# Eight chunks' loads, issued from GpSimd's queue instead of SP's: a hybrid decoder block

## The chip, the cores and the metric

The kernel runs on one core of one Trainium2 chip. The metric is the time of one execution on the device in microseconds (us), median of several runs. The core has five engines with a queue of instructions each: TensorE (PE in the profile, its weight loads PEld), VectorE (DVE), ScalarE (ACT), GpSimd (POOL) and SyncE (SP). A transfer between HBM and SBUF is issued by an instruction on one of the queues and carried out by 16 DMA engines. SBUF is the memory that the engines work in, PSUM the one that TensorE writes to.

## The reference

One layer over 2048 positions of width 1024, all in float32:

```python
h = rmsnorm(x, norm1_g[l])
proj = h @ w_in[l]
p_q, p_k, p_v, p_g, p_a, c_b, c_c, c_h = jnp.split(proj, splits, axis=-1)
...
o = gla_chunked(q, k, v, log_a)              # gated linear attention, 4 heads
o = rmsnorm(o, gla_norm_g[l]).astype(x.dtype)
o_gla = (o * jax.nn.silu(p_g...)).reshape(bsz, seq, GLA_WIDTH)
u = c_c * c_h
o_conv = c_b * causal_depthwise_conv(u, conv_w[l])
mixed = jnp.concatenate([o_gla, o_conv], axis=-1) @ w_out[l]
x = x + mixed
h2 = rmsnorm(x, norm2_g[l])
ffn = (jax.nn.silu(h2 @ w_ffn_gate[l]) * (h2 @ w_ffn_up[l])) @ w_ffn_down[l]
return rmsnorm(x + ffn, norm_f_g)
```

The attention works on chunks of positions. In each chunk q and k are scaled with exponentials of the summed log decays, scores of q and k are masked and multiplied with v, and a state (per head 64 x 128) is carried from chunk to chunk:

```python
q_i = q * jnp.exp(b)
k_i = k * jnp.exp(-b)
scores = jnp.where(causal, jnp.einsum('nbhck,nbhsk->nbhcs', q_i, k_i), 0.0)
o = jnp.einsum('nbhcs,nbhsv->nbhcv', scores, v) + jnp.einsum('nbhck,nbhkv->nbhcv', q_i, state_prev)
```

## The kernel before

Positions are cut into four blocks of 512 (`PB`), two to a half. Large products run on operands split into a high and a low part (`split`, lines 206 and 207: ACT rounds to the high part, DVE subtracts for the low one), three matmuls for one (lines 504 to 506), and by a scheme with seven block products for eight (`PRODUCTS`, `unit`). Weights come in as `raw` tiles and are added, split into `wq` tiles (four buffers) and multiplied.

The stages in order: the input projection of half 0, that of half 1, the first output projection (`first_out_proj`, half 0), the second (`out_proj`, half 1), then the feed-forward part for both halves.

Attention runs beside the projections. The kernel uses chunks of 128 positions, eight to a half. The input projection writes q and k, the summed log decays, v and the gate of each chunk to scratch tensors in DRAM (`s_kq`, `s_d`, `s_v`, `s_g`). `gla_half(half)` is a generator which fetches them back and works through the chunks; each call of `tick()` in the projections takes one of its steps. A chunk goes through these steps:

- `gla_fetch` (line 1156) takes four tiles `kq`, `ee`, `vt`, `gt` from the pool `bx`, and issues four loads through `load` (line 156), which is SP's queue: ee (128 KB), kq, vt and gt (256 KB each).
- `gla_scaled` takes two exponentials on ACT (lines 1163 and 1164) and scales k and q on DVE (1165 and 1166).
- `gla_scores` makes the scores on TensorE (1176) and masks them on DVE (1179), and transposes k and v (1182, 1185).
- `gla_outputs` multiplies (1201, 1208), makes the chunk's share of the state (1216 on TensorE, 1226 and 1227 on DVE) and the norm, and scales the outputs into a tile `osb` of the same pool (1242).
- `gla_finish` transposes, multiplies with the gate (1252), splits and stores to `s_gla` (line 1257).

The pool `bx` has 11 buffers (line 74). Chunk n+1 is fetched behind the scores of chunk n and ahead of the finish of chunk n-1. The tile `gt` is held until the finish; `kq`, `ee` and `vt` are free after lines 1208 and 1216.

The second half's chunks are fetched from the later part of half 1's input projection on, through `first_out_proj`. There the operands of the output projection are loaded too (`mix_operands`, line 1316: tiles `op`), with weights (`raw`), residuals (`y`, line 1339) and stores of results, all on SP's queue. In `first_out_proj` each product is added to the residual on DVE (`plus`, line 1366), and the first two rows of results are squared on ACT (`sum_squares`, line 1271).

No order is written down for most of this. The program is traced in the order of the Python code, which sets priorities, and a planner then orders each queue at build time by a model's times and hands out buffers and semaphores (line 1965):

```python
with _tile.TileContext(nc, schedule_with_timeline_sim=True) as tc:
    tile_hymba_block(tc, *args)
```

At run time each queue is carried out in the planned order; an instruction waits for its semaphores, and what stands behind it waits too. Some places fix an order by hand (`behind`, `tc.issue_after`, `queued`), among them the table load ahead of the first chunk (line 1130).

GpSimd's queue holds ten multiplications at the very end (line 1739) and a few fills at the start, and no DMA.

Of the kernel before, what the change touches and what calls it, by code (L numbers as in the profile page):

```python
# [54 lines left out]
def tile_hymba_block(ctx, tc, x, xt, win, wa, wgu, wout, wffn, wdown, wdown_first, small, out):  # L55
    nc = tc.nc
    act, dve, pool, pe = nc.scalar, nc.vector, nc.gpsimd, nc.tensor
# [95 lines left out]
    def bt(name, shape=(P, PB)):  # L153
        return bx[0].tile(list(shape), F32, name=name, tag="b")

    def load(dst, src):
        return nc.sync.dma_start(dst, src)
# [970 lines left out]
    def gla_half(half):  # L1128
        chunks = [(b, t) for b in (2 * half, 2 * half + 1) for t in range(PT)]
        with tc.issue_after(last_silu[0].ins):  # L1130
            tables = act.preload_act_table_set("natural_log_exp_and_others")
        fetched = gla_fetch(*chunks[0])
        yield
        with tc.issue_after(tables.ins):
            cur = gla_scaled(*fetched)
        yield
        o = None
        for n, (b, t) in enumerate(chunks):
            s = gla_scores(b, t, *cur)
            yield  # L1140
            if n + 1 < len(chunks):
                fetched = gla_fetch(*chunks[n + 1])
            if o is not None:
                yield from gla_finish(*chunks[n - 1], *o)
            o = gla_outputs(b, t, *s)
            if n + 1 < len(chunks):
                cur = gla_scaled(*fetched)
            yield
        yield from gla_finish(b, t, *o)
        done.add((b, t))  # L1150
        yield
# [4 lines left out]
    def gla_fetch(b, t):  # L1156
        kq, e, vt, g = [bt(n, (P, 4, P)) for n in ("kq", "ee", "vt", "gt")]
        for dst, src in ((e[:, 2:4, :], s_d), (kq[:], s_kq), (vt[:], s_v), (g[:], s_g)):
            load(dst, src[b][:, t])
        return kq, e, vt, g  # L1160

    def gla_scaled(kq, e, vt, g):
# [807 lines left out]
```

## Time and profile before

| | |
|---|---|
| median of 3 runs | 2032.9 us (2032.5 to 2035.67) |
| the profiled execution | 2031.92 us, its span 2030.0 us |
| granted TensorE clock, mean | 0.997 |
| busy: PE, PEld, DVE, ACT, POOL | 2011.4, 1654.4, 1564.8, 973.1, 10.3 us |
| DMA | 425.12 MB, mean 209 GB/s; all but 5 issues of the program on SP's queue |
| loads of the chunks (both halves) | kq, vt, gt: 16 issues each of 256 KB, landing after 4.7, 4.7 and 4.8 us (medians); ee: 16 of 128 KB, 4.8 us |

Times in the profile count from the first instruction. A line of a timeline gives start, duration, engine, line of the code, operation, `out<-in` by the program's names, and the count of instructions merged into it; a bracket behind it is idle time of that engine and what ended it. `SPq` marks an issue on SP's queue, whose duration is that of issuing; the time to landing is given apart. A line of a table by stretches gives for each engine its busy time and count, then the granted clock as a share (PEclk), the mean busy share of the 16 DMA engines (it can come out a little above 1), and GB/s. In the view of waits, `A <- B: total, times, longest` says how long A stood idle until B released it. In the view of a tile, three numbers are the smallest, the median and the largest duration in ns.

### The profile page before, as it was taken

Reading aid. Unit: us, or ns where it says so; the run is one execution under the profiler, and the core shown is the slowest. Engines: PE = TensorE matmul, PEld = TensorE weight load, DVE = VectorE, ACT = ScalarE, POOL = GpSimd, SP = SyncE. Lnnn points to the kernel's source line nnn. Section 1 sums busy time; section 2 is a strip of 40 time slices with the busy share of each in tenths; the row PEclk is TensorE's granted clock in tenths of the full one; section 3 lists DMA queues with packets and bytes.
Section 4 is the critical chain, followed back from the end, with each engine's and each line's share of the span. In section 5 each row is a group of like instructions: output and inputs, shape, how many; then the busy total and the mean of one; then the engine's idle time right before and its main releaser. Section 6 shows DMA issues by size and latency. Waiting matters only on the chain.

```text
span 2030.0 us, 26783 instructions
## 1 busy us (share of the span) xinstructions
PE 2011.4 (99%) x9275; PEld 1654.4 (81%) x9275; DVE 1564.8 (77%) x2837; ACT 973.1 (48%) x1941; POOL 10.3 (1%) x17
## 2 busy tenths in 40 slices
PE   9999999999999999999999999999999999999998
PEld 8888888788878888888888888887888888888886
DVE  7888868677867877877876687887767767778886
ACT  6664455754544444444444552334434444454345
POOL 0000000000000000000000000000000000000001
PEclk9999999999999999999999999999999999999999
DMA  7366876654777863545544676586444434586653
GB/s 264 117 200 215 288 278 207 184 171 138 262 272 256 293 232 130 181 169 199 182 163 174 233 283 246 186 286 268 171 151 171 174 132 171 183 331 217 249 218 130
DMA packets 191943, 425.12 MB, mean 209 GB/s; under 512 B 17760, under 2 KB 67136, under 8 KB 182336
## 3 DMA queue, kind: packets, MB, share of 16 engines
q1 hardware_dynamic: 191088, 422.76, 59.1%
q8 instruction: 73, 1.20, 0.2%
q10 hardware_dynamic: 720, 0.66, 0.1%
q14 instruction: 62, 0.51, 0.1%
HBM read 277.60 MB, written 145.75 MB: 209 GB/s over the span
## 4 chain that ended last, share of the span: by engine, by line
PE 96%; DMA 1%; DVE 1%; ACT 1%; issue 0%; SPq 0%; POOL 0%; POOLq 0%; DVEq 0%; ACTq 0%
PE mm L504 27%; PE mm L506 27%; PE mm L505 27%; PE mm L1395 1%; PE mm L1437 1%; PE mm L1439 1%; PE mm L1436 1%; PE a_ps L1028 1%; PE mm L809 1%; PE mm L811 1%; PE mm L810 1%; PE o_ps L1201 1%; PE mm L1401 1%; PE mm L1756 1%; PE sc L1176 1%; PE o_ps L1208 1%
## 5 line engine op out<-in xcount | busy, mean ns | idle before, releaser
L504 PE MATMUL mm<-op,wq 128*128 128x512 f32 x2499 | 973.0, 392 | 2.2 <-ACT c L550 1.4
L505 PE MATMUL mm<-op,wq 128*128 128x512 f32 x2499 | 972.0, 390 | 0.1
L506 PE MATMUL mm<-op,wq 128*128 128x512 f32 x2499 | 961.2, 390 | 0.3
L206 ACT ACTIVATE wq<-raw 128x512 fp32r<-128x512 f32 (+2 forms) x628 | 361.9, 581 | 596.3 <-PE mm L506 487.0
L504 PEld LDWEIGHTS mm<-op,wq 128*128 128x128 f32 x2499 | 469.0, 188 | 105.1 <-ACT wq L206 2.5
L506 PEld LDWEIGHTS mm<-op,wq 128*128 128x128 f32 x2499 | 469.1, 188 | 99.1 <-DVE wq L207 1.1
L505 PEld LDWEIGHTS mm<-op,wq 128*128 128x128 f32 x2499 | 469.2, 188 | 97.4 <-DVE op L207 2.0
L207 DVE TENSOR_TENSOR wq<-raw,wq 128x512 fp32r<-128x512 f32 (+2 forms) x628 | 390.1, 626 | 150.6 <-ACT wq L206 149.2
L538 DVE TENSOR_TENSOR c<-mm,c 128x512 f32<-128x512 f32 x196 | 134.7, 687 | 76.4 <-PE mm L506 71.4
L538 DVE TENSOR_TENSOR y<-mm,y 128x512 f32<-128x512 f32 x185 | 126.5, 686 | 52.0 <-PE mm L506 51.6
L550 ACT ACTIVATE c<-mm 128x512 f32<-128x512 f32 x198 | 115.6, 588 | 28.8 <-PE mm L506 26.2
L456 DVE TENSOR_TENSOR raw<-raw 128x512 f32<-128x512 f32 (+2 forms) x190 | 116.6, 619 | 2.1
L206 ACT ACTIVATE wq<-s 128x512 fp32r<-128x512 f32 (+2 forms) x100 | 58.0, 580 | 110.3 <-PE mm L506 96.5
L456 DVE TENSOR_TENSOR s<-raw 128x512 f32<-128x512 f32 (+2 forms) x95 | 58.9, 620 | 28.0 <-DMA raw<-in_wffn_dram 18.6
L207 DVE TENSOR_TENSOR op<-op 128x512 fp32r<-128x512 f32 x108 | 70.6, 682 | 1.9 <-ACT op L206 1.9
L206 ACT ACTIVATE op<-op 128x512 fp32r<-128x512 f32 x108 | 63.1, 621 | 10.1 <-DMA op<-sa_T 4.4
L207 DVE TENSOR_TENSOR wq<-s,wq 128x512 fp32r<-128x512 f32 (+2 forms) x100 | 62.4, 624 | 1.8 <-ACT wq L206 1.0
L456 DVE TENSOR_TENSOR raw<-s,raw 128x512 f32<-128x512 f32 (+2 forms) x95 | 59.0, 621 | 1.4
L605 ACT ACTIVATE sg<-mm 128x512 f32<-128x512 f32 x26 | 15.5, 597 | 87.6 <-PE mm L506 87.6
L605 ACT ACTIVATE c<-c 128x512 f32<-128x512 f32 x78 | 48.9, 628 | 13.0 <-DVE c L538 10.4
L1436 PE MATMUL mm<-op,wq 128*128 128x512 f32 x128 | 50.0, 392 | 0.0
L1437 PE MATMUL mm<-op,wq 128*128 128x512 f32 x128 | 49.8, 389 | 0.0
(238 smaller groups left out, 1665.4 us busy)
## 6 DMA issues: line engine op xcount, KB each, us to landing
raw<-in_wffn_dram SPq DMA_DIRECT2D x44, 1024.0 KB, 6.6
sa_B<-so SPq DMA_DIRECT2D x47, 512.0 KB, 4.1
op<-sa_B SPq DMA_DIRECT2D x47, 512.0 KB, 7.0
raw<-in_win_dram SPq DMA_DIRECT2D x22, 1024.0 KB, 5.7
sa_T<-so SPq DMA_DIRECT2D x44, 512.0 KB, 4.4
op<-sa_T SPq DMA_DIRECT2D x44, 512.0 KB, 6.8
raw<-in_wdown_dram SPq DMA_DIRECT2D x24, 768.0 KB, 5.5
sx<-y SPq DMA_DIRECT2D x48, 256.0 KB, 3.6
```

What stands on the lines that cost most here:

```text
L206: last_hi[:] = [act.activation(hi, src, AF.Copy)]
L207: last_lo[:] = [dve.tensor_tensor(lo, src, hi.bitcast(F32), ALU.subtract)]
L456: dve.tensor_tensor(*args)
L504: pe.matmul(o[:], wh, xh, start=first and k == 0, stop=False, skip_group_check=True)
L505: pe.matmul(o[:], wh, xl, start=False, stop=False, skip_group_check=True)
L506: return pe.matmul(o[:], wl, xh, start=False, stop=k == n - 1, skip_group_check=True)
L538: last_plus[:] = [dve.tensor_tensor(t[:], o[:], t[:], ALU.add)]
L550: last_out[:] = [act.activation(t[:], o[:], AF.Copy)]
L605: last_silu[:] = [act.activation(s[:], c[:], AF.Silu)]
L809: pe.matmul(acc[:], wq[:, 0, c], p[:, 0, :], start=first, stop=False)
L1436: pe.matmul(o[e, j][:], wh, m[:, 0, :], start=n == 0, stop=False)
L1437: pe.matmul(o[e, j][:], wh, m[:, 1, :], start=False, stop=False)
```

## The change

In `gla_fetch` the four loads of a chunk of blocks 2 and 3, the second half, are issued with `pool.dma_start`, on GpSimd's queue. The first half's stay on SP's. That is 32 of the 64 chunk loads. Tiles, sources and the place in the traced program are the same; the planner makes its order anew.

```diff
@@ -1156,7 +1156,10 @@
     def gla_fetch(b, t):
         kq, e, vt, g = [bt(n, (P, 4, P)) for n in ("kq", "ee", "vt", "gt")]
         for dst, src in ((e[:, 2:4, :], s_d), (kq[:], s_kq), (vt[:], s_v), (g[:], s_g)):
-            load(dst, src[b][:, t])
+            if b < 2:
+                load(dst, src[b][:, t])
+            else:
+                pool.dma_start(dst, src[b][:, t])
         return kq, e, vt, g
```

## The prediction, on record before the changed kernel ran

> **What bounds the kernel now.** I read the page first: the span, the busy times and the chain that ended last.
>
> ```profile
> span 2030.0 us, 26783 instructions
> PE 2011.4 (99%) x9275; PEld 1654.4 (81%) x9275; DVE 1564.8 (77%) x2837; ACT 973.1 (48%) x1941; POOL 10.3 (1%) x17
> PE 96%; DMA 1%; DVE 1%; ACT 1%; issue 0%; SPq 0%; POOL 0%; POOLq 0%; DVEq 0%; ACTq 0%
> ```
>
> TensorE holds 96% of the chain and is busy for 2011.4 of 2030.0 us. A moved load can therefore pay only where TensorE stands still, 18.6 us in all, and only in the part of it that the second half's chunks cause. So next came a table by stretches over the time in which these chunks run, within 460 to 645 us.
>
> ```profile
> core 0: us, PE busy (x) PEld busy (x) DVE busy (x) ACT busy (x) POOL busy (x), PEclk, DMA share, GB/s
> 500.00:536.00 36.00, 36.00 (x208) 29.34 (x207) 28.12 (x64) 23.60 (x63) 0.00 (x0) 1.00 0.43 133
> 536.00:556.00 20.00, 20.00 (x114) 16.33 (x113) 18.18 (x44) 10.17 (x31) 0.00 (x0) 1.00 0.99 380
> 556.00:570.00 14.00, 14.00 (x77) 11.21 (x76) 9.75 (x25) 5.12 (x19) 0.00 (x0) 1.00 1.05 398
> 570.00:575.00 5.00, 0.67 (x3) 0.21 (x2) 4.52 (x11) 3.09 (x7) 0.00 (x0) 0.98 1.00 351
> 575.00:580.00 5.00, 4.88 (x24) 4.23 (x25) 1.57 (x5) 1.82 (x4) 0.00 (x0) 0.68 1.08 392
> 580.00:600.00 20.00, 20.00 (x111) 15.99 (x110) 13.73 (x33) 8.27 (x25) 0.00 (x0) 1.00 0.69 223
> ```
>
> One hole shows, at 570 to 575, and behind it a stretch of 5 us at a granted clock of 0.68. Before and after, TensorE is full at clock 1.00. From 536 to 580 the DMA engines are full too (share 0.99 to 1.08): the operands of the first output projection come in there. The view of waits, over 460 to 645 us, for TensorE alone and then for all engines:
>
> ```profile
> PE sc L1176 <- DVE kq L1166: 4.4, 1, 4.4
> ```
>
> ```profile
> ACT ee L1163 <- DMA ee<-sd: 5.7, 4, 3.9
> DVE kq L1165 <- DMA kq<-sk: 4.7, 3, 2.1
> ```
>
> The hole is one wait of the scores of a chunk (the sixth of the second half) for its scaled q and k. Chunk loads do keep ACT (5.7 us) and DVE (4.7 us) waiting as well, but TensorE has no hole at those places, so there these waits cost nothing.
>
> **What ends the one hole.** The timelines of the four engines, put in order of time:
>
> ```profile
> 570.06 0.61 PE L1401 MATMUL mm<-op,wq 128*128 128x512 f32 x2
> 571.46 1.28 DVE L1366 TENSOR_TENSOR y<-mm,y 128x512 f32<-128x512 f32 x2
> 572.17 1.23 ACT L1271 ACTIVATE ssx<-y 128x512 f32<-128x512 f32 x2 [1.04 <-DVE y L1366]
> 573.44 0.42 ACT L206 ACTIVATE wq<-raw 128x256 fp32r<-128x256 f32 x1
> 573.76 0.40 ACT L1163 ACTIVATE ee<-ee 128x256 f32<-128x256 f32 x1
> 574.19 0.42 ACT L1164 ACTIVATE ee<-ee 128x256 f32<-128x256 f32 x1
> 574.23 0.42 DVE L1165 TENSOR_TENSOR kq<-kq,ee 128x256 f32<-128x256 f32 x1
> 574.64 0.42 DVE L1166 SCALAR_TENSOR_TENSOR kq<-kq,ee 128x256 f32<-128x256 f32 x1
> 575.12 1.23 PE L1176 MATMUL sc<-kq 64*128 64x128 f32 x8 [4.44 <-DVE kq L1166]
> ```
>
> ```profile
> 566.50 0.32 SPq L157 DMA_DIRECT2D ee<-sd  x1
> 567.24 0.32 SPq L157 DMA_DIRECT2D kq<-sk  x1
> ```
>
> The ee load, issued at 566.50, landed after 4.9 us, and kq's, issued at 567.24, after 6.5 us, by the view of each tile held to these two issues:
>
> ```profile
> DMA to landing us min/median/max: 4.9/4.9/4.9
> ```
>
> ```profile
> DMA to landing us min/median/max: 6.5/6.5/6.5
> ```
>
> So ee was there at 571.4 and kq at 573.7, both before their first reader (573.76 and 574.23). No row of the chain carries a wait for a DMA. What TensorE waits for is the order on ACT and DVE: two residual additions (L1366) that need its last product, two squares (L1271), one weight split (L206), and only then the exponentials (L1163, L1164) and the scaling (L1165, L1166).
>
> **What the change removes.** 8 chunks by 4 loads, 32 issues on SP. Medians from the views of the tiles:
>
> ```profile
> L157 SPq DMA_DIRECT2D ee<-sd x16: 319/524/1668, 288.9 to 593.4; - x16
> L157 SPq DMA_DIRECT2D kq<-sk x16: 319/404/646, 289.6 to 593.8; - x16
> ```
>
> With the two other loads at kq's price that is 0.52 + 3 x 0.40 = 1.7 us a chunk, 14 us of SP over 130 us. SP is not on the chain (0%), so the saving itself is worth nothing. What stood behind these loads on SP (operand loads, weights, stores of finished chunks) goes out sooner. No TensorE wait ends on one of those either, so this too counts 0; the cover is TensorE's full stretches above.
>
> **What it moves.** On SP a chunk's loads stand in program order behind everything else. The sixth chunk's come out at 566.50, though the products that last read the buffers of the fourth chunk's ee, kq and vt end near 548.3:
>
> ```profile
> 547.00 0.71 PE L1208 MATMUL o_ps<-carry,kq 64*128 64x128 f32 x8
> 547.65 0.66 PE L1216 MATMUL kv<-vt,ee 128*64 128x128 f32 x8
> ```
>
> If the planner gives the sixth chunk these buffers, GpSimd can issue its loads from about 548 on: estimated 18 us earlier. The bytes stay the same and the 16 engines are full, so the loads overtake other traffic and make no room.
>
> ```profile
> kq<-sk SPq DMA_DIRECT2D x16, 256.0 KB, 4.7
> ee<-sd SPq DMA_DIRECT2D x16, 128.0 KB, 4.8
> ```
>
> Three loads of kq's size and ee are 0.9 MB; at 398 GB/s they put 2.3 us in front of operands already queued. Those are read by products in a stretch where TensorE shows no wait; I take 0, and 2.3 us as the other end.
>
> **What it adds.** 32 issues on GpSimd, and for each consumer a wait on a semaphore of another queue. GpSimd has nothing else between these two rows:
>
> ```profile
> 1.41 0.41 POOL L83 TENSOR_SCALAR_AFFINE_SELECT mask<-mask 128x256 f32<-128x256 f32 x1
> 2014.19 7.06 POOL L1739 TENSOR_TENSOR y<-y,ssx 128x512 f32<-128x512 f32 x7 [2012.38 <-ACT ssx L1733]
> ```
>
> No row shows a load issued there. The nearest are its own operations, 0.41 us and 7.06/7 = 1.01 us. Then ee and kq are out after 0.8 to 2.0 us, against 0.9 us on SP, and all four after 1.6 to 4.0 us. [...] Where a chunk has no lead, 1.1 us (2.0 less 0.9) would show. Queued behind a waiting load on GpSimd are only loads of later chunks, until 2014 us.
>
> [...]
>
> **The sum.** The profiled execution took 2031.92 us (span 2030.0), 1 us below the median of three runs, 2032.9. Removed from the path 0, moved 0, added 0: while ACT and DVE keep their order, the wait of 4.44 us stays, since an earlier kq waits in SBUF until ACT comes to L1163. That gives 2031.92 for this execution and 2032.9 us for the median. About 0.2%, 4.1 us, is what a measurement of this kernel can tell from no change.
>
> **Rival: the planner moves the exponentials forward (faster).** The order on every queue is planned when the program is built, from a model's times, and a load on an idle queue has another time in it. ACT has room ahead of the hole:
>
> ```profile
> 569.58 0.73 ACT L206 ACTIVATE wq<-raw 128x256 fp32r<-128x256 f32 x2 [2.37 <-PE mm L506]
> ```
>
> The two exponentials (0.82 us) fit into these 2.37 us of idle, DVE has 4.25 us free in 556 to 570 for the scaling, and TensorE would go on at 570.67. Gone are 4.44 us and the slow clock behind it, 5.00 x (1 - 0.68) = 1.6 us: 6.04 us, 2026.9 us. For it: the loads can come 18 us earlier. Against: full DMA engines hold back the modelled arrival too, whichever queue issues.
>
> **Rival: another order, another hole (slower).** Scores are placed with no reserve: the fifth chunk's ran at 548.24, one tenth of a microsecond after its scaling.
>
> ```profile
> 547.73 0.41 DVE L1166 SCALAR_TENSOR_TENSOR kq<-kq,ee 128x256 f32<-128x256 f32 x1
> 548.24 0.71 PE L1176 MATMUL sc<-kq 64*128 64x128 f32 x8
> ```
>
> If the new plan counts on earlier loads and puts the scores of the fifth or seventh chunk further forward, while DVE (18.18 of 20 us busy in 536 to 556) gets to the scaling as late as now, TensorE stops there as it does at 570. It decides from the point where the scores come up before the end of L1166. Each such stop, priced as the one there is, costs 6.04 us: 2038.9, and 2045.0 with two. For it: DVE is the second busiest engine and just there nearly full. Against: the present plan has only one such stop in eight chunks.
>
> **Rival: GpSimd in DVE's way (slower).** The end of the kernel is the one place where both work on SBUF:
>
> ```profile
> 2011.03 0.17 DVE L1708 TENSOR_TENSOR rs<-py 128x4 f32<-128x4 f32 x1 [0.45 <-ACT py L1705]
> 2015.45 1.29 DVE L1708 TENSOR_TENSOR rs<-py 128x2 f32<-128x2 f32 x1
> ```
>
> The same operation took 0.17 us alone and 1.29 us beside GpSimd's products, 1.12 us more. At that price for each load, the 8 loads of the fifth and sixth chunks cost DVE 9.0 us; 1.8 us are idle in 536 to 556, and the other 7.1 us would reach TensorE: 2040.0 us. Against: GpSimd reads tensors at 2015 and would not for a load.
>
> [...]
>
> **How the numbers follow.** No change to speak of, 2032.9: 0.29. Exponentials forward, 2026.9: 0.26. New holes, 2038.9 to 2045.0: 0.27. GpSimd against DVE, 2040.0 or worse: 0.18. Forecast 2032.9 us, its own range 2032.5 (the lowest run) to 2035.2 (2.3 us for overtaken operands). With the others: from 2026.0, the lowest run 2032.5 less 6.04, rounded down, to 2045.0; a third hole or a dearer GpSimd lies outside. Faster 0.26, same 0.29, slower 0.45.
>
> **What would show it.** Right, if the 32 loads stand on GpSimd's queue, the waits of ACT and DVE for ee and kq shrink from 5.7 and 4.7 us to near nothing, the sixth chunk's loads land many microseconds before L1163, and TensorE still waits some 4.4 us for L1166 behind the two L1271. Wrong to the fast side, if L1163 stands ahead of L1271 and the hole and the 0.68 stretch are gone. Wrong to the slow side, if there are more waits of sc for kq, if operations of DVE are stretched while GpSimd issues, or if a landing from GpSimd's queue takes clearly longer than 4.9 to 6.5 us.

## The result and the profile after

The changed kernel takes 2037.84 us, the kernel before 2032.57 us (medians of 16 executions each). The ratio is 1.0023, 95% interval 1.0017 to 1.003: slower by 5 us. The ratio on record is an estimate of its own and not the quotient of the medians, which is 1.0026; so it is with the ratios below. Three slow executions, of 2547.07, 5402.24 and 6934.36 us, are left out of all medians and ratios below. The forecast was 2032.9 us, no change, with 2032.5 to 2035.2 as its own range. The executions of the changed kernel also lie further apart, 2034.25 to 2041.9 us, where 14 of the 16 of the kernel before lie within 2031.45 to 2033.6. The profiled execution of the changed kernel took 2034.3 us, one of its shortest, so its trace shows only a part of the loss; two more executions were profiled for that reason. Behind `gla_fetch` the line numbers are 3 higher than before.

The page of the changed kernel, its span, busy times, DMA queues and the chain:

```profile
span 2032.6 us, 26832 instructions
...
PE 2013.0 (99%) x9275; PEld 1656.8 (82%) x9275; DVE 1565.8 (77%) x2837; ACT 973.5 (48%) x1941; POOL 27.5 (1%) x49
...
q0 software_dynamic: 2304, 7.34, 1.2%
q8 instruction: 73, 1.20, 0.2%
...
q14 instruction: 64, 0.52, 0.1%
...
PE 97%; DVE 1%; DMA 1%; ACT 1%; issue 0%; POOL 0%; POOLq 0%; SPq 0%; ACTq 0%
```

The 32 loads are a queue of their own now (q0). Two more queues matter below, of the kind that the page calls `instruction`: q8 with packets of 16 KB (1.20 MB / 73) and q14 with packets of 8 KB (0.52 MB / 64). They are read here as fetches of the engines' instructions.

The table by stretches, to be set against the one of before:

```profile
536.00:556.00 20.00, 19.16 (x106) 14.99 (x105) 17.35 (x41) 9.91 (x29) 1.60 (x3) 1.00 0.99 384
556.00:570.00 14.00, 14.00 (x78) 11.18 (x77) 9.93 (x27) 5.46 (x18) 2.05 (x4) 1.00 1.05 393
570.00:575.00 5.00, 1.96 (x9) 1.30 (x7) 3.88 (x9) 2.90 (x7) 0.09 (x1) 1.00 1.00 387
575.00:580.00 5.00, 3.82 (x20) 3.22 (x21) 3.49 (x9) 2.34 (x6) 0.54 (x1) 0.73 0.75 262
```

The one hole of before is still there, and so is the slow clock behind it (0.73). The order that makes it is the one foreseen, here from the timelines of ACT, DVE and TensorE:

```profile
572.90 0.63 ACT L1274 ACTIVATE ssx<-y 128x512 f32<-128x512 f32 x1 [0.48 <-DVE y L1369]
573.83 0.63 ACT L1274 ACTIVATE ssx<-y 128x512 f32<-128x512 f32 x1 [0.30 <-DVE y L1369]
574.50 0.42 ACT L206 ACTIVATE wq<-raw 128x256 fp32r<-128x256 f32 x1
574.82 0.40 ACT L1166 ACTIVATE ee<-ee 128x256 f32<-128x256 f32 x1
...
575.70 0.42 DVE L1169 SCALAR_TENSOR_TENSOR kq<-kq,ee 128x256 f32<-128x256 f32 x1
576.18 0.71 PE L1179 MATMUL sc<-kq 64*128 64x128 f32 x8 [4.22 <-DVE kq L1169]
```

The sixth chunk's loads are out 18 us earlier (GpSimd's timeline). They land after 6.2 us (ee) and 7.0 us (kq), at 554.8 and 556.4 us, 20 and 19 us ahead of their readers. Over the whole second half the median time to landing is shorter than before, but most loads are issued at other times (the view of DMA from 430 to 645 us, first the changed kernel, then the one before):

```profile
548.55 0.54 POOL L1162 DMA_DIRECT2D ee<-sd  x1 [22.74 <-PE o_ps L1211]
549.35 0.54 POOL L1162 DMA_DIRECT2D kq<-sk  x1 [0.27 <-ACT wq L206]
```

```profile
kq<-sk POOLq DMA_DIRECT2D x8, 256.0 KB, 5.1
...
ee<-sd POOLq DMA_DIRECT2D x8, 128.0 KB, 3.7
```

```profile
kq<-sk SPq DMA_DIRECT2D x8, 256.0 KB, 6.8
...
ee<-sd SPq DMA_DIRECT2D x8, 128.0 KB, 5.1
```

**Where the time goes.** Not in the chunks. Each trace has 9275 matmuls, so their start times can be compared one by one with those of the kernel before (2031.92 us). Between its 1378 and 1394 us the changed kernel falls back by 1.4 us in the first profile (2034.3 us), by 3.1 in `again1` (2035.21) and by 5.8 in `again2` (2037.78); between 540 and 600 us, where the chunks run, by 0.7, 0.5 and 0.7 us; behind 1394 us by 0.1 at most. Some 800 us after the chunks, in the feed-forward part, TensorE stands still at 1384 to 1393 us, where it did not before (the same view of the kernel before has no row). The waits of TensorE from 1380 to 1400 us in the first profile (2034.3 us) and in the longest one taken (2037.78 us, `again2`), and that one's stretch behind the hole:

```profile
PE mm L504 <- ACT op L206: 1.0, 1, 1.0
PE mm L505 <- DVE op L207: 0.2, 1, 0.2
```

```profile
PE mm L504 <- ACT op L206: 2.3, 1, 2.3
PE mm L504 <- DMA op<-shB: 1.3, 1, 1.3
PE mm L505 <- DVE op L207: 0.2, 1, 0.2
```

```profile
1390.00:1400.00 10.00, 7.48 (x25) 5.36 (x24) 6.30 (x10) 5.97 (x10) 0.00 (x0) 0.83 0.98 344
```

In `again2` that is 3.8 us of holes and 10.00 x (1 - 0.83) = 1.7 us of slow clock, 5.5 us: the size of the median loss. The operands that come late there are `op` tiles loaded by SP. One split on ACT that TensorE waits for in `again2` is held up by this load, issued at 1377.53 us before and at 1382.40 us in `again2`:

```profile
1377.53 0.32 SPq L157 DMA_DIRECT2D op<-shT  x1
```

```profile
1382.40 0.32 SPq L157 DMA_DIRECT2D op<-shT  x1
...
1392.52 0.63 ACT L206 ACTIVATE op<-op 128x512 fp32r<-128x512 f32 x1 [2.72 <-DMA op<-shT]
```

SP falls behind at 1350 to 1361 us. SP's timeline, the kernel before and the changed one (first profile):

```profile
1349.84 0.32 SPq L157 DMA_DIRECT2D y<-sx  x1
1350.47 0.32 SPq L163 DMA_DIRECT2D sx<-y  x1
1353.65 0.32 SPq L157 DMA_DIRECT2D op<-shB  x1
1354.07 0.38 SPq L163 DMA_DIRECT2D sx<-y  x1
1358.33 0.32 SPq L157 DMA_DIRECT2D op<-shB  x1
```

```profile
1350.42 0.32 SPq L157 DMA_DIRECT2D y<-sx  x1
1351.06 0.32 SPq L163 DMA_DIRECT2D sx<-y  x1
1355.23 0.32 SPq L157 DMA_DIRECT2D op<-shB  x1
1355.95 0.32 SPq L163 DMA_DIRECT2D sx<-y  x1
1360.68 0.32 SPq L157 DMA_DIRECT2D op<-shB  x1
```

Each `op` load waits here until the store issued just before it has landed: a store landing after 3.2 us lets SP go on at 1353.65, one landing after 4.2 us at 1355.23. From the first of these five issues to the last SP needs 8.5 us before and 10.3 after. SP's order in this place is the same in both kernels. Issue for issue, SP's lag against the kernel before grows from 0.6 to 2.4 us over these five in the first profile. It is down to 0.4 us at the `op` load of 1363.27 us, but that load then takes 8.4 us to land instead of 5.9, and from the `op` load of 1368.04 to that of 1384.55 us the lag is 2.9 us (3.7 to 4.9 in `again2`; 0.2 in `half_b` and 0.1 to 0.3 in `pad_dve`, two kernels of the experiments without the loss). What differs at the start of it is seen in the DMA engines from 1350 to 1355 us (the row of GB/s in 40 slices, and the queues), before and after; the load and the store are issued 0.6 us later in the second:

```profile
GB/s 328 475 361 410 360 393 410 393 426 360 492 360 442 344 442 377 410 426 377 475 328 475 295 262 82 98 0 0 0 0 0 0 0 0 0 0 33 229 131 33
...
q1 hardware_dynamic: 642, 1.25, 71.0%
```

```profile
GB/s 492 393 393 360 459 475 311 410 377 393 410 377 443 344 459 361 459 328 442 377 459 344 492 360 377 393 311 279 98 66 16 0 33 16 33 16 33 16 0 0
...
q1 hardware_dynamic: 683, 1.42, 73.5%
q14 instruction: 1, 0.01, 0.5%
```

Before, the flow breaks off at once. After, it trails off over a microsecond at 16 to 33 GB/s, few packets at a time, and the load and the store land only then. In that window there is one packet on q14 that the kernel before does not have there, an 8 KB fetch of instructions, which by the trace's records began at 1352.85 us. In the kernel before, the corresponding fetch began at 1357.5.

**Fetch theory.** The loads' consumers now wait for a semaphore of one more queue. Some of these waits take an instruction of their own: the trace counts 606 semaphore instructions on DVE instead of 600 and 679 on ACT instead of 670, and 32 loads fewer on SP. With them the fetches of instructions move, and one of DVE's now meets the load and the store on which SP's run of round trips hangs. The rivals, named in the expectations: the new order of TensorE in the chunks (order), loads that overtake operands (traffic), or a GpSimd load that is dear wherever it stands (queue).

The view of one line shows it in place: the line that multiplies with `gt` has 8 semaphore instructions before and 11 after.

```profile
L1252 DVEq EVENT_SEMAPHORE  x8: 21/21/21, 329.1 to 639.1; - x8
```

```profile
L1255 DVEq EVENT_SEMAPHORE  x11: 21/21/50, 328.9 to 640.3; - x11
```

### The profile page after: what moved, and what is told of

It is laid out like the page before. It is cut to its first block, busy times and chain, and to the rows that moved or that the text cites. A ratio compares the mean times of both kernels' runs of the same rounds, so it can differ in the third digit from the quotient of the medians.

```text
span 2032.6 us, 26832 instructions
## 1 busy us (share of the span) xinstructions
PE 2013.0 (99%) x9275; PEld 1656.8 (82%) x9275; DVE 1565.8 (77%) x2837; ACT 973.5 (48%) x1941; POOL 27.5 (1%) x49
## 4 chain that ended last, share of the span: by engine, by line
PE 97%; DVE 1%; DMA 1%; ACT 1%; issue 0%; POOL 0%; POOLq 0%; SPq 0%; ACTq 0%
PE mm L504 28%; PE mm L506 27%; PE mm L505 27%; PE mm L1398 1%; PE mm L1439 1%; PE mm L1442 1%; PE mm L1440 1%; PE mm L809 1%; PE a_ps L1028 1%; PE mm L811 1%; PE mm L810 1%; PE mm L1404 1%; PE mm L1759 1%; PE o_ps L1204 1%; PE sc L1179 1%; PE o_ps L1211 1%
## 5 line engine op out<-in xcount | busy, mean ns | idle before, releaser
L207 DVE TENSOR_TENSOR wq<-raw,wq 128x512 fp32r<-128x512 f32 (+2 forms) x628 | 391.6, 628 | 149.1 <-ACT wq L206 147.9
L207 DVE TENSOR_TENSOR op<-op 128x512 fp32r<-128x512 f32 x108 | 71.3, 688 | 3.9 <-ACT op L206 3.9
L207 DVE TENSOR_TENSOR wq<-s,wq 128x512 fp32r<-128x512 f32 (+2 forms) x100 | 62.6, 626 | 1.8 <-ACT wq L206 1.0
```

The source lines that it names most:

```text
L207: last_lo[:] = [dve.tensor_tensor(lo, src, hi.bitcast(F32), ALU.subtract)]
```

## The experiments

Each kernel is compared with the kernel before run beside it (medians 2032.4 to 2032.9 us). The prices in the traces are those of one execution each.

**1. The changed kernel again.**

> The changed kernel once more, for a second profile, because its 16 times spread from 2034.3 to 2041.9 us and the first profile (2034.3 us) is near the lowest. Order theory (the plan's new order of TensorE between 545 and 575 us costs the time): the same holes as in the first profile, 4.2 us at 572 and under 1 us elsewhere. Traffic theory (loads of the fifth to eighth chunk go out early and overtake operands of the output projection): other holes between 525 and 580 us, ended by an op tile or a weight that landed late, and their sum grows with the time. Queue theory (a load issued by GpSimd is dear wherever it stands): extra holes beside each group of GpSimd issues, also at 441 to 511 us.

> The changed kernel a third time, for a profile of one of its longer executions. Fetch theory: what is longer is the hole at 1390 us (1.0 us in the 2034.3 us execution, 2.7 us in the 2035.2 us one), with the landings of the run of stores and loads at 1350 to 1361 us; the stretch from 440 to 600 us is the same. Queue theory: the holes of the stretch from 440 to 600 us.

Measured: 2035.21 and 2037.78 us. The holes from 1380 to 1396 us come to 2.9 and 3.9 us (1.25 in the first profile). The hole in the chunks is 4.2 us in all three; the small one at 537 us, 0.64 in the first profile, is missing in both. The loss is not made in the chunks, which is what the fetch theory had said of `again2`.

**2. Parts of the change.** The condition in `gla_fetch` decides which chunks go to GpSimd.

```diff
-            if b < 2:
+            if b != 2:            # half_a;   half_b: b != 3;   chunk5: (b, t) != (3, 0)
                 load(dst, src[b][:, t])
```

> Only the first four chunks of the second half (block 2) are loaded from GpSimd's queue, 16 loads at 440 to 511 us; TensorE's planned order is that of the kernel before. Order theory: no change, 2032.6 us. Traffic theory: no change, 2032.6, since the 16 DMA engines are not full before 524 us. Queue theory: half of the 5.3 us, 2035.2 us.

> Only the last four chunks (block 3) are loaded from GpSimd's queue, 16 loads from 523 us on; TensorE's planned order is that of the changed kernel. Order theory and traffic theory: the whole loss, 2037.8 us, with the same spread of several us between executions. Queue theory: half, 2035.2 us.

> Only the fifth chunk's four loads are issued from GpSimd's queue; that alone gives TensorE's planned order of the changed kernel, number for number. Order theory: the whole loss, 2037.8 us. Traffic theory: a part, as one of four chunks overtakes operands: 2033.5 to 2035. Queue theory: an eighth, 2033.2 us.

Measured: half_a 2033.32 us (ratio 1.0002, 0.9993 to 1.0011), half_b 2032.48 (1.0001, 0.9992 to 1.001), chunk5 2033.85 (1.0004, 0.9995 to 1.0012). None has a measurable loss. half_b has the whole new order of TensorE (its matmuls stand in the changed kernel's order, one by one) and all the overtaking loads, and its interval ends at 1.001, 2 us: neither order nor traffic makes the 5 us. chunk5's median lies in the range that the traffic theory gave (2033.5 to 2035), but half_b has four times its loads and lies lower. Together the halves lose 0.7 us by their medians (against 2032.55), not 5, which speaks against a price per load, though the intervals would allow up to 4. By the traces each half adds three semaphore instructions on DVE, not six, and its fetch begins at 1354.2 and 1353.4 us, when the load has landed.

**3. Streams made longer by hand.** Fills of one element on DVE and loads of 4 bytes on SP, with no other queue's order touched:

```diff
+    pad = const.tile([P, 64], F32, name="pad")
 ...
+    load(pad[0:1, at : at + 1], small[0:1, at : at + 1])      # pad_sp, pad_both: 32
+    dve.memset(pad[0:1, 32 + at : 33 + at], 0.0)              # pad_dve, pad_both: 24
```

> The changed kernel with 32 loads of 4 bytes added on SP's queue during the second output projection (600 to 700 us), so that SP has its old count of issues again from there on; every other queue keeps its order. Fetch theory (the change shortened SP's and lengthened DVE's instruction stream, which moved two 8 KB instruction fetches to 1352.9 and 1358.2 us, into a run of stores and loads on SP that each wait for the one before): SP's fetch moves from 1358 back to about 1330 us, DVE's stays at 1352.9, the hole at 1390 us shrinks, time between 2033 and 2036. Queue theory and traffic theory (the loss is made where GpSimd's loads run, before 600 us): no effect, 2037.8 us.

> The changed kernel with 24 fills of one element added on DVE's queue during the second output projection; every other queue keeps its order. Fetch theory: DVE's fetch moves from 1352.9 to about 1340 us, SP's stays at 1358, the landings of the store and load at 1350.4 to 1351.4 are 1 us quicker, time between 2033 and 2036. Queue theory and traffic theory: no effect, 2037.8 us.

> The changed kernel with both paddings, 32 loads of 4 bytes on SP and 24 fills on DVE. Fetch theory: both fetches are out of the way, the hole at 1390 us is at most 0.3 us, and the time is 2032.6 to 2033.5 with the narrow spread of the kernel before. Queue theory and traffic theory: no effect, 2037.8 us.

> The kernel before with six fills of one element added on DVE's queue during the second output projection, and no load moved: DVE's instruction stream is as long there as that of the changed kernel. Fetch theory: DVE's fetch moves from 1357.5 to about 1352.9 us, the store and load issued at 1350 land 1 us later, SP falls back by 1 us, and part of the loss appears, 2033 to 2035, although GpSimd issues no load. Queue theory and traffic theory: 2032.6 us.

One thing in these expectations did not hold: with nothing to wait for, the fills were planned to the head of DVE's queue (2.6 to 3.0 us) and the small loads early on SP's (32 to 52 us), more than 1280 us ahead of DVE's fetch, which came at 1338.7 us in pad_dve and at 1340.6 in pad_both, against 1352.9 in the changed kernel. The added tile raises the line numbers by one. Measured: pad_sp 2037.42 us (1.0023, 1.0013 to 1.0032), pad_dve 2033.78 (1.0006, 0.9998 to 1.0015), pad_both 2033.57 (1.0002, 0.9993 to 1.0011). SP's longer queue takes nothing back; 24 idle instructions on DVE take back 4 of the 5 us. The kernel before with six fills and all loads on SP takes 2035.86 us (1.0013, 1.0005 to 1.0022): more than half of the loss without one load on GpSimd. The fetch theory had expected an effect of pad_sp as well; by pad_sp's time (2037.42 us, the changed kernel 2037.84) SP's own fetch at 1358.2 us is of no account.

SP's timeline in pad_dve, the fetch now at 1338.7 us, is back to the old steps:

```profile
1350.21 0.32 SPq L158 DMA_DIRECT2D y<-sx  x1
...
1354.05 0.32 SPq L158 DMA_DIRECT2D op<-shB  x1
...
1358.69 0.32 SPq L158 DMA_DIRECT2D op<-shB  x1
```

**4. Only this fetch.** The fills of experiment 3 stood at 2.6 to 3.0 us, some 1350 us ahead of the fetch. Here they are tied behind an addition in the kernel before, where they stand at 1325 us (the expectation said about 1310):

```diff
+                if last and half == 0 and d0 == 0:
+                    with behind(all_plus[-1:]):
+                        for i in range(6):        # bef_late2: 2, bef_late9: 9
+                            dve.memset(pad[0:1, i : i + 1], 0.0)
```

> The kernel before with six fills of one element on DVE's queue, tied behind an addition at about 1310 us, so that DVE's stream is unchanged up to there (in the earlier padded kernels the fills stood at the head of DVE's queue and moved all of DVE's fetches). Every other queue keeps its order. Fetch theory with the place named (the fetch of DVE that lands at 1352.9 instead of 1357.5): the same loss as with six fills at the head, 2035 to 2036. If another of DVE's fetches makes the loss (one between 440 and 600 us, where the chunks run): 2032.7, no loss.

> The kernel before with two fills instead of six at the same place (about 1310 us). By the rows of DVE's timeline the fetch then falls about four instructions later than with six, at 1354 to 1355.5 us, behind the landing of the load and store issued at 1349.8 and 1350.5 (1353.0 and 1353.6). Position theory (it matters whether the fetch meets that load and store): no loss to speak of, 2032.5 to 2034. Count theory (each added instruction ahead of 1350 costs): a third of the 3 us, 2033.8.

> The kernel before with nine fills at that place. The fetch then comes three instructions earlier than with six, at about 1350.4 us, where the load and the store have just been issued and the transfers ahead of them still run. Position theory: the load and store are met as well, 2034.5 to 2036; if the engine makes the 0.3 us good before they end, 2032.8. Count theory: 2037.4.

Measured: two fills 2033.24 us (1.0001, 0.9992 to 1.001), six 2035.83 (1.0016, 1.0007 to 1.0025), nine 2036.46 (1.0018, 1.0008 to 1.0027). Everything up to 1325 us is that of the kernel before, so the loss is made behind it. With nine the loss lies between what the two theories gave, and the fetch came at 1352.2 us, not at the expected 1350.4: a still earlier place was not reached. That 24 fills take most of the loss away (pad_dve) speaks against the count. TensorE's wait with six fills:

```profile
PE mm L505 <- ACT op L207: 2.0, 1, 2.0
PE mm L506 <- DVE op L208: 0.2, 1, 0.2
```

The profiled executions up to here together, worked out from the traces (start of the fetch on q14; time from the issue of `y<-sx` at about 1350 us to that of the first `op<-shB`, and on to the second; holes of TensorE from 1380 to 1396 us):

| kernel | execution, us | fetch | first step | second step | holes |
|---|---|---|---|---|---|
| before | 2031.92 | 1357.5 | 3.8 | 4.7 | 0.0 |
| chunk5 | 2032.17 | 1354.0 | 3.8 | 4.6 | 0.0 |
| half_b | 2032.17 | 1353.4 | 3.8 | 4.8 | 0.2 |
| bef_late2 | 2032.65 | 1353.5 | 3.8 | 4.5 | 1.2 |
| pad_dve | 2032.84 | 1338.7 | 3.8 | 4.6 | 0.1 |
| half_a | 2033.63 | 1354.2 | 4.2 | 4.8 | 0.4 |
| pad_both | 2035.95 | 1340.6 | 3.8 | 4.6 | 1.4 |
| bef_dve6 | 2032.52 | 1351.4 | 4.7 | 4.7 | 0.8 |
| after | 2034.3 | 1352.9 | 4.8 | 5.5 | 1.3 |
| bef_late9 | 2036.33 | 1352.2 | 4.9 | 5.4 | 1.6 |
| bef_late6 | 2035.48 | 1351.7 | 4.8 | 6.0 | 2.3 |
| pad_sp | 2035.42 | 1352.8 | 5.2 | 5.8 | 2.5 |
| again1 | 2035.21 | 1352.7 | 5.1 | 6.5 | 2.9 |
| again2 | 2037.78 | 1352.0 | 4.8 | 6.0 | 3.9 |

The first step parts the kernels cleanly: 4.2 us at most where the fetch falls away from 1351 to 1353, 4.7 us at least where it falls there. Counted from the issue of `y<-sx`, that is 2.1 to 2.8 us behind it; in the others the fetch starts ahead of that issue or at least 3.7 us behind it. The hole varies from execution to execution, and the changed kernel's three profiles follow it (1.3, 2.9 and 3.9 us of holes in 2034.3, 2035.21 and 2037.78 us); up to 1.4 us of it come without the fetch too. Compared matmul by matmul with the kernel before, the seven executions with the fetch in that place lose 1.0 to 5.8 us between 1378 and 1394 us, the six others 0.0 to 1.6.

That the fetch is DVE's can be counted. When it starts, DVE has begun 2352 to 2357 of the instructions that its trace records, in 16 of the 17 profiles of this case; it is 2353 in the kernel before and in the changed one, where six more instructions bring the same count 4.65 us earlier. ACT stands at 1817 to 1833 then, SP anywhere from 1340 to 1401. The exception is `v3_sp` of experiment 5, with 2371.

One row of the table needs a remark: pad_both's execution, its longest, has a hole of 1.6 us at 537 us as well; its median is 2033.57 us.

**5. What the early loads are good for.** The sixth chunk's exponentials and scaling are tied ahead of what stood before them at 570 us. `sixth` notes this chunk, the 14th of all; the weight splits "S2" and "A12" are tied as the squares are.

```diff
 def gla_scaled(kq, e, vt, g):
...
+    done_exp = act.activation(e[:, 2:4, :], e[:, 2:4, :], AF.Exp, scale=1.0 / 16.0)
+    if len(sixth) == 14:
+        sixth.append(done_exp)
...
+    scaled = dve.scalar_tensor_tensor(
...
+    if len(sixth) == 15:
+        sixth.append(scaled)
...
 def sum_squares(ssq, y, first):
...
+    with behind(sixth[14:15] if sixth[14:15] != [None] else []):
         act.activation(ssq[:], y, AF.Square)
...
 def plus(at, o):
+    with behind(sixth[15:16] if d0 == 0 and len(sixth) == 16 else []):
         summed = dve.tensor_tensor(y[at][:], o[:], y[at][:], ALU.add)
```

> The changed kernel with 24 fills at the head of DVE's queue, and with the sixth chunk's exponentials and scaling ordered ahead of two squares and three weight splits on ACT and of the two additions, three splits and one subtraction on DVE that stood before them at 570 us. TensorE's, SP's and GpSimd's order stay. As the sixth chunk's loads now land before 558 us, the hole of 4.2 us at 571 us and the slow clock behind it (1.4 to 1.6 us) should go: 2033.8 less 5.6 to 5.8, 2028.0 us. Rival: the scores then wait for PSUM banks that the two additions free, 2 us are left: 2030 to 2031.

> The same reordering and fills with the loads of the second half on SP's queue as in the kernel before. There the sixth chunk's ee landed at 571.4 and kq at 573.7 us. If the early landing is what makes the reordering pay: ACT now stands still until ee is there, scaling ends near 574.5, TensorE's hole stays at 3 to 4.5 us and other products may wait for the splits behind it: 2032 to 2036 us. If the early landing is not needed: 2027 to 2028 us, as with the loads on GpSimd.

> The changed kernel with the reordering of the sixth chunk's exponentials and scaling, without the 24 fills. Fetch theory: the gain of the reordering stays, and the fetch meets the load and store again, so that the loss of 3 to 5 us by the hole at 1385 us comes on top of 2027.0: 2030 to 2032. If the fills did nothing there: 2027.0.

Measured: v3p (loads on GpSimd, 24 fills) 2027.0 us (0.9972, 0.9962 to 0.9982), quicker than both kernels; v3 (without the fills) 2030.21 (0.9988, 0.9978 to 0.9997); v3_sp (loads on SP, with the fills) 2033.76 (1.0002, 0.9993 to 1.0011). ACT's and TensorE's rows of v3p and then of v3_sp:

```profile
567.76 0.41 ACT L1172 ACTIVATE ee<-ee 128x256 f32<-128x256 f32 x1
568.19 0.42 ACT L1173 ACTIVATE ee<-ee 128x256 f32<-128x256 f32 x1
```

```profile
PE sc L1189 <- DVE kq L1177: 0.7, 1, 0.7
```

```profile
572.48 0.42 ACT L1172 ACTIVATE ee<-ee 128x256 f32<-128x256 f32 x1 [4.39 <-DMA ee<-sd]
```

```profile
PE sc L1189 <- DVE kq L1177: 3.0, 1, 3.0
```

With the loads from GpSimd the exponentials run in ACT's idle time and 0.7 of 4.2 us is left. With the loads on SP, ACT stands still for 4.39 us until ee is there, and 3.0 us are left. The median of v3_sp does not show this price by itself: the profiled execution, its longest (2036.45 us), has a fetch at 1352.3 us and 2.5 us of holes at 1390 too. Compared matmul by matmul with the kernel before, the two losses can be told apart: between 540 and 600 us v3p and v3 gain 4.4 us each and v3_sp 0.0; between 1378 and 1394 us v3p loses 1.2 us, v3 3.7 and v3_sp 4.2. The 3.2 us between the medians of v3 and v3p are the fetch's price again, though their intervals just touch: in v3 the first step, now at 1345 us, has the fetch 2.9 us behind its start and takes 5.2 us, in v3p the fetch is 11.6 us ahead and it takes 4.0 us.

## Why the prediction was wrong

- **The bound, and the hole that stays: right.** TensorE's hole is 4.22 us (4.44 before), behind the same two squares and the split on ACT. ACT and DVE wait no more for ee or kq (5.7 and 4.7 us before; no such row in the changed kernel from 460 to 645 us), and it gained nothing.
- **The move: right.** ee goes out at 548.55 instead of 566.50 us, the 18 us that were estimated. The landings are longer there (6.2 us for ee and 7.0 for kq, 4.9 and 6.5 before), which was to be a sign of the slow side, but with a lead of 19 us they cost nothing.
- **The issue on GpSimd: inside its range, without effect.** 0.54 us each, between the 0.41 and the 1.01 us of GpSimd's own operations; the sixth chunk's ee and kq were out after 1.3 us (548.55 to 549.89), where the range was 0.8 to 2.0. No run ahead of the result showed the 0 that the sum has for it; the leads of 20 and 19 us measured here bear it out. The shorter medians to landing (3.7 against 5.1 us, 5.1 against 6.8) do not show a quicker queue, as the loads go out at other times. In six pairs of the same load, issued within 0.15 us of each other before and after (at 496 and at 509 to 511 us), GpSimd's lands from 0.05 us sooner to 0.9 us later, 0.4 us later in the median.
- **What it adds: the step that failed.** The prediction named "for each consumer a wait on a semaphore of another queue" and put nothing against it in the sum. In its own place each costs some 21 ns (the median in the view of line 1255) of an engine with room. But some are instructions of their own, and six more of them on DVE shift a fetch by about 5 us (from 1357.5 to 1352.85), 800 us later. The term "added 0" should have read about 3 us, which is what six idle instructions cost the kernel before (bef_late6: 2035.83 against 2032.79). Why the changed kernel loses 5 us by its median and these six fills 3 is open; in the traces both lose it in the same place (1.4 to 5.8 and 3.9 us between 1378 and 1394 us).
- **The cover.** "TensorE's full stretches above" covered 460 to 645 us. The prediction did not look at what the change shifts outside of it, and neither did a rival or one of its signs of the slow side.
- **Rival, exponentials forward.** The planner did not do it; done by hand it gives 2027.0 us, where the rival said 2026.9. That they meet within 0.1 us is in part chance, as 0.7 us of the hole stayed and 24 fills were needed as well.
- **Rival, another order, another hole.** TensorE's order did change (12 matmuls went ahead of the fifth chunk's scores), and half_b has that order at 2032.48 us: no price.
- **Rival, GpSimd in DVE's way.** Not seen. The splits on DVE (L207) take 628 ns on average, 626 before, and half_b with 16 loads beside the busiest stretch loses nothing. No load of the six pairs above came more than 0.9 us later, with DVE busy for 3.0 of 4 us there (508 to 512 us).

The measured 2037.84 us lie outside the forecast's own range, 2032.5 to 2035.2. They lie inside the wide one that takes in the rivals, 2026.0 to 2045.0, and on the slower side, which had the larger chance (0.45), but that is luck: none of the rivals that made up that side came true, and the cause was not among them. The loss of 5 us is also more than the 4.1 us that the prediction took as the least that can be told from no change.

## What to carry to other kernels

A change that leaves the bound alone can still move an instruction fetch of an engine (DVE's here, from 1357.5 to 1352.85 us); where SP runs a chain of store, wait, load with little reserve, compare the fetch queue's packets of both traces before blaming the moved work. Comparing the two traces matmul by matmul shows in which 20 us the time is lost. Loads that arrived early paid here only when their first reader was ordered early too: the move alone lost 5 us, with the reordering and the 24 fills it gained 5.8. Where a wider spread of executions comes with a loss, profile a long execution; the first profile here showed a third of the hole that the longest had (1.25 of 3.9 us).

## What the hardware showed

- A fetch of instructions among the transfers that the kernel waits for goes with a later landing. In the profiles with the fetch in that place, those of v3 and v3_sp included, one 8 KB packet of 0.3 to 0.8 us goes with a 256 KB load that lands after 4.1 to 4.6 us; with the fetch elsewhere it lands after 3.2 to 3.5 us (the traces of pad_sp and pad_both give no landing). Why about 1 us and not 0.4, the packet's own time in the changed kernel, is not shown by any run.
- The fetches on q8 are 16 KB here and fit TensorE, whose trace has 18692 instructions, 256 for each of 73 packets. Those on q14 are 8 KB, and on SP they come about 128 instructions apart (with 850, 978, 1103, 1231 and 1361 of SP's instructions begun, in the changed kernel's trace): half the size, and twice as many for the same number of instructions.
- Two losses of 3 us and more (bef_late6, bef_late9) came from idle instructions of 59 ns each that no one waits for. That the fetch is DVE's follows from these runs: instructions on DVE move it (six fills from 1357.5 to 1351.7 us in bef_late6), 32 more on SP do not (1352.8 us in pad_sp, 1352.9 in the changed kernel). The exact rule by which a fetch starts stays open: with 24 fills at the head of DVE's queue it moved by 14 us in pad_dve, but a fetch stood at 1352.3 us in v3_sp, which has the same fills.
